# A hybrid decoder layer on one core: another order of the seven products of Strassen's scheme in the feed-forward part, with four of them summed in PSUM

## The chip, the cores and the metric

The kernel runs on 1 core of one Trainium2 chip. The metric is the device time of one execution in microseconds (us); a profile of one execution shows what each engine did. The engines are TensorE (PE; its weight loads are shown apart as PEld), VectorE (DVE), ScalarE (ACT), GpSimd (POOL) and SyncE (SP, which issues most transfers).

## The reference

One decoder layer on 512 positions of width 2048, in float32. The token mixers in the first half are not touched by the change; the feed-forward part is.

```python
D_MODEL, SEQ = 2048, 512
D_FF = 5632                         # -(-(8 * D_MODEL) // (3 * 256)) * 256
def reference(...):
    h = _rms_norm(x, norm1_g[l])
    proj = h @ w_in[l]
    ...                             # three causal token mixers: out_a, out_b, out_c
    x = x + jnp.concatenate([out_a, out_b, out_c], axis=-1) @ w_out[l]
    h2 = _rms_norm(x, norm2_g[l])
    x = x + (jax.nn.silu(h2 @ w_gate[l]) * (h2 @ w_up[l])) @ w_down[l]
```

## The kernel before

**Stages.** The input projection and the mixers come first, then the output projection, then an Up phase (gate and up) and a Down phase. All matrix products run in three passes: each float32 operand is split into a high part of reduced precision (`wh`, `high`) and the rest (`wl`, `low`), and high x high, high x low and low x high are summed in PSUM.

**Output projection.** It takes 32 units of work, each with one weight tile of 128x1024 and 24 matmuls of 512 columns. A unit writes one of two PSUM banks (pool `tiles`); `residual` (L1098) adds the bank to the residual `xr` on DVE. With each finished row of x, small steps follow by a clock of ticks: the square on ACT (L1118) and its sum `ssum` on DVE (L97), and the halves of the normalised activations, their differences and sums (`ta`, `tb`, `h`, L1128 to L1148), which the Up phase multiplies. The last unit of the output projection is unit -1 here, the one ahead of it -2, and so on.

**Up and Down.** Both use a scheme of seven products in place of eight (Strassen's, in Winograd's form): the weights are cut into four quarters 11, 12, 21, 22, the activations likewise, and seven products of sums of quarters give the four quarters c00, c01, c10, c11 of the result. Up has 11 blocks of two sub-blocks, u0 to u21; one sub-block computes its seven products in the order of `ORDER`, each in two units A and B of 12 matmuls. The result quarters with first index 1 are the gate, those with 0 are up. Down has 12 blocks d0 to d11, of seven products too; where a range has three columns of blocks instead of four, the block is narrower (18 matmuls to a product instead of 24). A product fills two PSUM banks; there are two such pairs of banks, taken in turn, and the list `(7, 1, 5, 2)` says which products start a sum there afresh. A product outside the list adds to what is in its pair: 4 to product 7, 6 to product 1, 3 to product 5. `done` then tells what is read from the banks after each product and added to which result quarter; DVE does most of it, `six` reads product 6's sum three times.

**Weight sums.** Five sums of weight quarters are made on POOL by `plus` (L172), each in the raw buffers that the quarters were loaded to: s = 21 + 11; 21 = 21 + 22; 11 = 21 + 11 (with the new 21); and later 11 = 11 + 12, so four sums for each of A and B. The table `sums` puts each of them at the start of a numbered unit, counted from the first unit `base` of the sub-block. `entries` is the order of the loads, `bufs` says which raw buffer each quarter takes, and `pump` issues the next load as soon as its buffer is free. `works` is the order in which units use them. Two units ahead of its use, a quarter is split: ACT makes a rounded copy in PSUM (`wn`, L283) and one in SBUF (`wh`, L284), DVE subtracts (`wl`, L285). For the weights of the output projection DVE subtracts a copy in SBUF (L263).

The order of the work on each engine is that in which the program is written; no scheduler moves it.

## Time and profile before

| | |
|---|---|
| Time, median of 3 runs | 1843.49 us (1842.29 to 1843.87) |
| Span of the profiled execution | 1840.0 us |
| Its own time beside the span | not given apart; the median lies 3.49 us above the span |
| Output projection's last unit | 571.06 to 576.50 us |
| Up phase | 576.50 to 1414.30 us |
| Down phase | from 1414.30 us to near the end |

How its lines are read: a row of a timeline gives the start, the length, the engine, the line of the program, the operation, output <- inputs, and in brackets the idle time before it with what ended it. A group's row gives the count, the busy time, the mean of one in ns, and the idle time ahead. A row of windows gives the stretch, its length, each engine's busy time with its instructions, then the granted clock of PE, the share of the DMA engines and GB/s.

### The profile page before, as it was taken

To read this page: it belongs to the slowest core of one execution; us is meant where nothing else is said; L and a number is where in the kernel's file an instruction comes from. 1 tells how busy PE (TensorE), PEld (TensorE's weight loads), DVE (VectorE), ACT (ScalarE), POOL (GpSimd) and SP (SyncE) were. 2 spreads that over 40 slices of the span, in tenths; PEclk is the share of its full clock that TensorE was granted. 3 is DMA by queue.
4 is the path that set the end of the run, shared out by engine and by line. 5 is a ranking of instruction groups with operands and counts; after the bars stand their busy time and mean duration, and the time that the engine had idled before them with its cause. 6 is when DMAs were issued, how large, how long until landed. Compare 5 with 4: busy or idle time off the path is not lost.

```text
span 1840.0 us, 26561 instructions
## 1 busy us (share of the span) xinstructions
PE 1832.2 (100%) x8314; PEld 1521.0 (83%) x8314; DVE 1430.0 (78%) x2023; ACT 1313.4 (71%) x1784; POOL 1019.0 (55%) x793
## 2 busy tenths in 40 slices
PE   9999999999999999999999999999999999999998
PEld 7888888888888888888888888888888888888887
DVE  6689888986689877777777777777777777777777
ACT  6355644553468788887888888888887778877775
POOL 0126543110003557886887767787776558776552
PEclk9999999999999999999999999999999999999999
DMA  7353255363343466777867778677687579877635
GB/s 276 88 150 121 88 145 156 107 178 132 118 138 104 115 160 183 203 205 183 227 179 210 209 185 224 174 207 210 178 273 255 200 232 294 252 259 259 237 121 109
DMA packets 401612, 337.81 MB, mean 184 GB/s; under 512 B 185408, under 2 KB 327872, under 8 KB 401472
## 3 DMA queue, kind: packets, MB, share of 16 engines
q1 hardware_dynamic: 400896, 335.33, 62.9%
q8 instruction: 66, 1.08, 0.2%
q10 hardware_dynamic: 576, 0.79, 0.1%
q14 instruction: 74, 0.61, 0.1%
HBM read 261.61 MB, written 66.03 MB: 178 GB/s over the span
## 4 chain that ended last, share of the span: by engine, by line
PE 73%; DVE 1%; DMA 0%; issue 0%; ACT 0%; DVEq 0%; SPq 0%
PE out L1307 15%; PE out L1304 15%; PE out L1306 15%; PE out L1570 7%; PE out L1569 7%; PE out L1571 7%; PE o L322 2%; PE o L324 2%; PE o L323 2%; DVE y L1579 0%; DVE wl L285 0%; DMA out_T<-z 0%; DVE z L1478 0%; DVE lnv L412 0%; DVE y L1548 0%
## 5 line engine op out<-in xcount | busy, mean ns | idle before, releaser
L1304 PE MATMUL out<-wh,h 128*128 128x512 f32 x1232 | 479.2, 389 | 0.0
L1306 PE MATMUL out<-wl,h 128*128 128x512 f32 x1232 | 479.2, 389 | 0.0
L1307 PE MATMUL out<-wh,h 128*128 128x512 f32 x1232 | 479.2, 389 | 0.0
L1306 PEld LDWEIGHTS out<-wl,h 128*128 128x128 f32 x1232 | 231.2, 188 | 48.1
L1307 PEld LDWEIGHTS out<-wh,h 128*128 128x128 f32 x1232 | 231.2, 188 | 48.1
L1304 PEld LDWEIGHTS out<-wh,h 128*128 128x128 f32 x1232 | 231.2, 188 | 47.9
L1570 PE MATMUL out<-wl,a 128*128 128x512 f32 x620 | 240.4, 388 | 0.1
L1569 PE MATMUL out<-wh,a 128*128 128x512 f32 x620 | 240.4, 388 | 0.0
L1571 PE MATMUL out<-wh,a 128*128 128x512 f32 x620 | 240.3, 388 | 0.0
L289 ACT CAST wh<-w 128x1024 fp32r<-128x1024 f32 (+2 forms) x94 | 97.0, 1031 | 134.3 <-PE o L323 46.0
L1579 DVE TENSOR_TENSOR y<-y,out 128x512 f32<-128x512 f32 x192 | 128.4, 684 | 46.8 <-PE out L1571 45.0
L263 DVE TENSOR_TENSOR wl<-w,wh 128x1024 fp32r<-128x1024 f32 (+2 forms) x95 | 114.4, 1204 | 34.0 <-ACT wh L289 33.8
L1570 PEld LDWEIGHTS out<-wl,a 128*128 128x128 f32 x620 | 116.4, 188 | 24.2 <-DVE wl L285 0.5
L1569 PEld LDWEIGHTS out<-wh,a 128*128 128x128 f32 x620 | 116.4, 188 | 24.1
L1571 PEld LDWEIGHTS out<-wh,a 128*128 128x128 f32 x620 | 116.4, 188 | 23.8
L573 DVE SCALAR_TENSOR_TENSOR y<-bu,cst,y 128x511 f32<-128x511 f32 (+14 forms) x120 | 88.9, 741 | 1.1
L322 PE MATMUL o<-mh_c,wh 128*128 128x512 f32 x128 | 51.0, 398 | 0.0
L322 PE MATMUL cq<-hh,wh 128*128 128x512 f32 x128 | 50.3, 393 | 0.0
L324 PE MATMUL o<-mh_c,wl 128*128 128x512 f32 x128 | 50.0, 391 | 0.0
L323 PE MATMUL o<-ml_c,wh 128*128 128x512 f32 x128 | 50.0, 390 | 0.0
L323 PE MATMUL cq<-hl,wh 128*128 128x512 f32 x128 | 49.9, 390 | 0.0
L324 PE MATMUL cq<-hh,wl 128*128 128x512 f32 x128 | 49.9, 390 | 0.0
(2353 smaller groups left out, 4745.0 us busy)
## 6 DMA issues: line engine op xcount, KB each, us to landing
od<-a SPq DMA_DIRECT2D x154, 256.0 KB
a<-od SPq DMA_DIRECT2D x154, 256.0 KB
w<-in_wi SPq DMA_DIRECT2D x58, 512.0 KB
w<-in_wo SPq DMA_DIRECT2D x32, 512.0 KB
x<-in_xT SPq DMA_DIRECT2D x16, 256.0 KB
xr<-in_xT SPq DMA_DIRECT2D x16, 256.0 KB
x2d<-xr SPq DMA_DIRECT2D x16, 256.0 KB
z<-x2d SPq DMA_DIRECT2D x64, 64.0 KB
```

The lines of the kernel that those rows point to most:

```text
L263: fn(*args)
L289: (nc.vector.tensor_copy if u == 0 else nc.scalar.copy)(hi[:, :n], t[:, :n])
L322: nc.tensor.matmul(out, wh, xh, start=start, stop=False)
L323: nc.tensor.matmul(out, wh, xl, start=False, stop=False)
L324: nc.tensor.matmul(out, wl, xh, start=False, stop=stop)
L1304: nc.tensor.matmul(b, x[:, high], wh[:, s], start=c == f == 0 and q in (7, 1, 5, 2), stop=False, skip_group_check=True)
L1306: nc.tensor.matmul(b, x[:, high], wl[:, s], start=False, stop=False, skip_group_check=True)
L1307: nc.tensor.matmul(b, x[:, low], wh[:, s], start=False, stop=c == f == 1, skip_group_check=True)
L1569: nc.tensor.matmul(b[:, lo:hi], x[:, high], wh[:, s], start=start, stop=False, skip_group_check=True)
L1570: nc.tensor.matmul(b[:, lo:hi], x[:, high], wl[:, s], start=False, stop=False, skip_group_check=True)
L1571: nc.tensor.matmul(b[:, lo:hi], x[:, low], wh[:, s], start=False, stop=last, skip_group_check=True)
L1579: getattr(eng, op)(t, t, src)
```

## The change

`ORDER` becomes 1, 7, 6, 4, 5, 2, 3, and only 1, 7 and 2 start afresh. So 6 is summed onto 1 in the same banks, 4 onto 7, 5 onto 1 + 6, and, after 2 in the other pair, 3 onto 1 + 6 + 5. Each pair of banks is read once after each product: `six` and, in Down, `copy_u` with its subtraction on POOL go away; c10 takes product 6's sum with a minus sign. The weight sums are placed anew: s three units ahead of the sub-block instead of four, 21 two units ahead instead of at its start, 11 one ahead instead of two behind; the last sum stays at the eighth unit. The loads come in the order 11, 21, 22, 12 instead of 21, 11, 22, 12, the buffers are shared out in another way, and 12 is loaded only once s has been made. Near the end of Down the transposes of result c10 come after product 4 instead of 6.

```diff
-ORDER = (7, 1, 4, 6, 5, 2, 3)
+ORDER = (1, 7, 6, 4, 5, 2, 3)
+FRESH = (1, 7, 2)
...
-    bufs = {"A": dict(zip(("21", "11", "s", "22"), ("21a", "22a", "sa", "22b"))),
-            "B": dict(zip(("21", "11", "s", "22"), ("21b", "11", "12", "sb")))}
+    bufs = {"A": dict(zip(("11", "21", "22", "s"), ("21b", "22a", "sa", "22b"))),
+            "B": dict(zip(("11", "21", "22", "s"), ("21a", "11", "12", "sb")))}
+
+    def use(base, size, keys, c):
+        i, key, buf = "AB".index(c), keys[c], bufs[c]["s"]
+        sums[base - 3 + i].append(plus(key["s"], key["21"], key["11"], size[c], buf))
+        sums[base - 2 + i].append(plus(key["21"], key["21"], key["22"], size[c]))
+        sums[base - 1 + i].append(plus(key["11"], key["21"], key["11"], size[c]))
+        sums[base + 7 + i].append(plus(key["11"], key["11"], key["12"], size[c]))
+
+    BLOCKS = (("11", False), ("s", True), ("11", False), ("22", True), ("21", True), ("12", True), ("11", True))
+
+    def turn_bufs():
+        return {c: {"11": b["22"], "21": b["21"], "22": b["s"], "s": b["11"]} for c, b in bufs.items()}
...
-        for k in ("21", "11", "22", "12"):
+        for k in ("11", "21", "22", "12"):
...
-            sums[base - 4 + i].append(plus(key["s"], key["21"], key["11"], 1024, bufs[c]["s"]))
-            sums[base + i].append(plus(key["21"], key["21"], key["22"], 1024))
-            sums[base + 2 + i].append(plus(key["11"], key["21"], key["11"], 1024))
-            sums[base + 7 + i].append(plus(key["11"], key["11"], key["12"], 1024))
-        works.extend((keys[c][k], last, "moves") for k, last in (
-            ("s", True), ("11", False), ("22", True), ("11", False), ("21", True), ("12", True), ("11", True)) for c in "AB")
+            use(base, {"A": 1024, "B": 1024}, keys, c)
+        works.extend((keys[c][k], last, "moves") for k, last in BLOCKS for c in "AB")
...
-        bufs = {c: {"21": b["22"], "11": b["21"], "s": b["s"], "22": b["11"]} for c, b in bufs.items()}
+        bufs = turn_bufs()
...
     def pump(limit, most=99, eng=nc.sync):
         while at["entry"] < len(entries) and len(raws) < limit and entries[at["entry"]][0] not in held and most:
+            key = entries[at["entry"]][1]
+            if isinstance(key, tuple) and key[0] == "12" and ("s", key[1]) not in made:
+                break
...
-        def six(self, by, a, b):
-            by(0, 1, a, b)
-            self.less(0, a, b)
-            self.less(1, a, b)
...
                 elif q == 6:
-                    if a:
-                        later(0, self.six, by, a, b)
-                    else:
-                        self.six(by, a, b)
+                    if first:
+                        self.keep(1, 0, a, b, -1.0)
+                    else:
+                        self.less(0, a, b)
...
-            if self.end:
-                self.less(1, 0, a, b)
-            else:
-                later(0, self.copy_u, a, b, queue=extras)
-
-        def copy_u(self, a, b):
-            u = slot(f"d{self.t}u{a}")
-            nc.scalar.copy(u, b)
-            later(0, self.less, 1, 0, a, u, nc.gpsimd)
...
-            if self.end and q == 6:
+            if self.end and q == 4:
```

How it moves instructions is seen best at three places. In the changed program the lines stand a few numbers lower down (L172 is L173 there, L285 L290, L1330 L1335, L1579 L1581 or L1585, L1478 L1480).

The first is POOL ahead of and in the first sub-block, u0. Before:

```order
L172 TENSOR_TENSOR w('s', 'u0A')_5765<-w('21', 'u0A')_5556,w('11', 'u0A')_5609 128x1024
L172 TENSOR_TENSOR w('s', 'u0B')_5814<-w('21', 'u0B')_5559,w('11', 'u0B')_5664 128x1024
L172 TENSOR_TENSOR w('21', 'u0A')_5556<-w('21', 'u0A')_5556,w('22', 'u0A')_5817 128x1024
L172 TENSOR_TENSOR w('21', 'u0B')_5559<-w('21', 'u0B')_5559,w('22', 'u0B')_5872 128x1024
L172 TENSOR_TENSOR w('11', 'u0A')_5609<-w('21', 'u0A')_5556,w('11', 'u0A')_5609 128x1024
L172 TENSOR_TENSOR w('11', 'u0B')_5664<-w('21', 'u0B')_5559,w('11', 'u0B')_5664 128x1024
```

After the change:

```order
L173 TENSOR_TENSOR w('s', 'u0A')_5818<-w('21', 'u0A')_5609,w('11', 'u0A')_5504 128x1024
L173 TENSOR_TENSOR w('21', 'u0A')_5609<-w('21', 'u0A')_5609,w('22', 'u0A')_5714 128x1024
L173 TENSOR_TENSOR w('s', 'u0B')_5873<-w('21', 'u0B')_5664,w('11', 'u0B')_5559 128x1024
L173 TENSOR_TENSOR w('11', 'u0A')_5504<-w('21', 'u0A')_5609,w('11', 'u0A')_5504 128x1024
L173 TENSOR_TENSOR w('21', 'u0B')_5664<-w('21', 'u0B')_5664,w('22', 'u0B')_5769 128x1024
L173 TENSOR_TENSOR w('11', 'u0B')_5559<-w('21', 'u0B')_5664,w('11', 'u0B')_5559 128x1024
```

The sum into 21 of A now stands ahead of s of B, and the first sum into 11 ahead of 21 of B. What the order doesn't show: s of A takes the buffer that unit -2's weights leave, s of B that of unit -1; before, these went to the two loads of 22, and s took buffers that were free earlier.

The second is DVE around product 6 in the first sub-block of an Up block (block 5; `out_5990` to `out_5993` are the four PSUM banks, `b5c` the result tiles). Before, from the reads of product 6 to those of product 5:

```order
L1330 TENSOR_TENSOR b5c_9776<-b5c_9776,out_5992 128x512
L1330 TENSOR_TENSOR b5c_9669<-b5c_9669,out_5992 128x512
L285 TENSOR_TENSOR wl_9840<-w('12', 'u10A')_9588,wn_9841 128x1024
L1319 TENSOR_SCALAR b5c_9865<-out_5993,n2w 128x512
L1330 TENSOR_TENSOR b5c_9778<-b5c_9778,out_5993 128x512
L1330 TENSOR_TENSOR b5c_9671<-b5c_9671,out_5993 128x512
L285 TENSOR_TENSOR wl_9870<-w('12', 'u10B')_9612,wn_9871 128x1024
L1330 TENSOR_TENSOR b5c_9669<-b5c_9669,out_5990 128x512
L1330 TENSOR_TENSOR b5c_9671<-b5c_9671,out_5991 128x512
```

After the change, from the read of product 6 past those of product 4 to those of product 5:

```order
L1322 TENSOR_SCALAR b5c_9735<-out_5991 128x512
L290 TENSOR_TENSOR wl_9741<-w('21', 'u10A')_9390,wn_9742 128x1024
L290 TENSOR_TENSOR wl_9772<-w('21', 'u10B')_9423,wn_9773 128x1024
L1329 TENSOR_TENSOR b5c_9733<-b5c_9733,out_5992 128x512
L1329 TENSOR_TENSOR b5c_9735<-b5c_9735,out_5993 128x512
L290 TENSOR_TENSOR wl_9798<-w('12', 'u10A')_9598,wn_9799 128x1024
L290 TENSOR_TENSOR wl_9827<-w('12', 'u10B')_9631,wn_9828 128x1024
L1335 TENSOR_TENSOR b5c_9681<-b5c_9681,out_5990 128x512
L1335 TENSOR_TENSOR b5c_9683<-b5c_9683,out_5991 128x512
```

Before, bank `out_5993` was read three times by DVE alone; now each bank has one reader (that of product 6's other bank is ACT's), and two adds follow two splits.

The third is DVE near the end, in the last Down block. Before, from the adds of product 6 (`x3`: three rows alike) to the first of product 5:

```order
L1579 TENSOR_TENSOR y<-y,out_5990 128x512 x3
L285 TENSOR_TENSOR wl_17767<-w('12', 'd11A')_17552,wn_17768 128x1024
L1478 STREAM_TRANSPOSE z_17761<-y 128x16x32
L1579 TENSOR_TENSOR y<-y,out_5991 128x512 x3
L1478 STREAM_TRANSPOSE z_17792<-y 128x16x32
L285 TENSOR_TENSOR wl_17795<-w('12', 'd11B')_17572,wn_17796 128x1024
L285 TENSOR_TENSOR wl_17817<-w('11', 'd11A')_17414,wn_17818 128x1024
L1478 STREAM_TRANSPOSE z_17792<-y 128x16x32
L1579 TENSOR_TENSOR y<-y,out_5992 128x512
```

After the change, from the adds of product 4, which has that place now, to the first of product 5:

```order
L1581 TENSOR_TENSOR y<-y,out_5990 128x512
L1581 TENSOR_TENSOR y<-y,out_5991 128x512
L290 TENSOR_TENSOR wl_17590<-w('12', 'd11A')_17418,wn_17591 128x1024
L1480 STREAM_TRANSPOSE z_17585<-y 128x16x32
L1480 STREAM_TRANSPOSE z_17612<-y 128x16x32
L290 TENSOR_TENSOR wl_17615<-w('12', 'd11B')_17438,wn_17616 128x1024
L290 TENSOR_TENSOR wl_17637<-w('11', 'd11A')_17206,wn_17638 128x1024
L1480 STREAM_TRANSPOSE z_17612<-y 128x16x32
L1585 TENSOR_TENSOR y<-y,out_5992 128x512
```

Of three adds to each bank one is left: four rows fewer ahead of the last splits.

## The prediction

> **What bounds the kernel now.** I read the page first, then the busy time by stage, then the lines that touch the change, and last the two places at which TensorE (PE) is not covered. The page:

> ```profile
> span 1840.0 us, 26561 instructions
> PE 1832.2 (100%) x8314; PEld 1521.0 (83%) x8314; DVE 1430.0 (78%) x2023; ACT 1313.4 (71%) x1784; POOL 1019.0 (55%) x793
> ```

> The span is 1840.0 us; the median of the runs, 1843.49, lies 3.49 above it, and I carry that offset unchanged. Matmuls fill the span. The busy time by stage (Up phase; Down phase to near the end; columns PE, PEld, DVE, ACT, POOL, then the granted clock):

> ```profile
> 576.50:1414.30 837.80, 837.80 (x3698) 693.71 (x3697) 643.80 (x741) 696.23 (x844) 614.16 (x420) 1.00 0.71 195
> 1414.30:1834.00 419.70, 419.51 (x1862) 347.37 (x1861) 320.72 (x382) 319.29 (x383) 265.00 (x161) 1.00 0.71 220
> ```

> In the Up phase PE has no gap at all, in the Down phase 0.2 us, at a clock of 1.00. DVE is busy 77% there, ACT 83%, POOL 73%, all beside PE. The change leaves the number of matmuls as it is, so work taken from DVE, ACT and POOL is worth nothing where PE doesn't wait; only a wait that goes or comes counts.

> **The change part by part.**

> *Fewer reads of products.* Groups and single rows of the adds:

> ```profile
> L1579 DVE TENSOR_TENSOR y<-y,out 128x512 f32<-128x512 f32 x192 | 128.4, 684 | 46.8 <-PE out L1571 45.0
> L1330 DVE TENSOR_TENSOR b1c<-b1c,out 128x512 f32<-128x512 f32 x12 | 7.8, 680 | 1.2 <-ACT b1c L1315 1.0
> 1437.26 0.57 ACT L1594 COPY d0u<-out 128x512 f32<-128x512 f32 x1
> 1437.91 1.30 POOL L1579 TENSOR_TENSOR y<-y,d0u 128x512 f32<-128x512 f32 x1 [5.80 <-ACT d0u L1594]
> ```

> Up loses 8 DVE operations per block, 11 x 8 x 0.68 = 60 us; Down loses 26 DVE adds (17.8 us), 22 ACT copies (12.5) and 22 POOL subtracts (28.6). All lay beside a full PE: price 0 but at the very end. The banks still alternate in pairs, each read while the other product's two units run, so no new bank wait arises.

> *The end.* DVE's last rows and PE's, in order of time:

> ```profile
> 1828.28 1.21 DVE L285 TENSOR_TENSOR wl<-w('11', 'd11B')_17437,wn 128x1024 fp32r<-128x1024 f32 x1
> 1829.08 0.39 PE L1569 MATMUL out<-wh,a 128*128 128x512 f32 x1
> 1829.54 0.50 PE L1570 MATMUL out<-wl,a 128*128 128x512 f32 x1
> 1829.88 0.40 PE L1571 MATMUL out<-wh,a 128*128 128x512 f32 x1
> ...
> 1831.82 0.65 DVE L1548 TENSOR_TENSOR y<-y,out 128x512 f32<-128x512 f32 x1
> 1832.52 0.44 PE L1534 MATMUL sides<-ident,y 128*128 128x128 f32 x2
> ...
> 1834.98 0.41 PE L1534 MATMUL sides<-ident,y 128*128 128x128 f32 x2 [0.60 <-DVE y L1548]
> ```

> At the pitch of 0.227 (837.8 us over 3696 matmuls: 11 blocks, 28 units, 12 each) the matmuls at 1829.54 and 1829.88 are 0.34 late, behind a weight split that DVE starts late, and the transposes at 1832.52 some 0.3 to 0.4 behind an add. In the last block DVE has four adds fewer ahead of that split (2.7 us), so both waits go: -0.7 (bounds 0 and -0.75). The last one (0.60) is a true dependence and stays.

> *The weight sums in the Up and Down phases.* They are POOL additions of 2.4 us. The new order wants the second sum into 11 made about 11.3 us after a sub-block's start T: product 6, which uses it, is moved one place ahead; its second unit starts at T + 5 x 2.72 = 13.6 and is split 2.3 earlier. The first sum can't start before T-9.1, when the previous block's last split has freed its buffer; until the second 11 sum POOL has six sums and at most a pair of gate products:

> ```profile
> 1260.45 2.41 POOL L172 TENSOR_TENSOR w('21', 'u18A')_12262<-w('21', 'u18A')_12262,w('22', 'u18A')_12478 128x1024 f32<-128x1024 f32 x1 [0.98 <-DMA w('22', 'u18A')_12478<-in_wgu]
> 1267.54 2.55 POOL L1386 TENSOR_TENSOR b8c<-b8c,b8c 128x512 f32<-128x512 f32 x2
> ```

> 6 x 2.41 + 2.55 = 17.0, so T+7.9: 3.4 us of cover. After a narrow Down block (28.56 us instead of 38.08, an estimate from 126 and 168 matmuls at 0.227) the same count, with the splits before it closer together, gives T+10.8: 0.5 of cover. Price 0, bounds 0 and +1.

> *The first sub-block.* Here the change costs. Before, its sums and the DVE rows beside them:

> ```profile
> 547.43 2.46 POOL L172 TENSOR_TENSOR w('s', 'u0A')_5765<-w('21', 'u0A')_5556,w('11', 'u0A')_5609 128x1024 f32<-128x1024 f32 x1 [68.13 <-DVE wl L263]
> 553.89 2.47 POOL L172 TENSOR_TENSOR w('s', 'u0B')_5814<-w('21', 'u0B')_5559,w('11', 'u0B')_5664 128x1024 f32<-128x1024 f32 x1 [4.00 <-DVE wl L263]
> 565.41 2.40 POOL L172 TENSOR_TENSOR w('21', 'u0A')_5556<-w('21', 'u0A')_5556,w('22', 'u0A')_5817 128x1024 f32<-128x1024 f32 x1 [9.05 <-DMA w('22', 'u0A')_5817<-in_wgu]
> 569.45 2.58 POOL L172 TENSOR_TENSOR w('21', 'u0B')_5559<-w('21', 'u0B')_5559,w('22', 'u0B')_5872 128x1024 f32<-128x1024 f32 x1 [1.64 <-DMA w('22', 'u0B')_5872<-in_wgu]
> ```

> ```profile
> 547.55 2.62 DVE L1148 TENSOR_TENSOR h<-h,h 128x256 fp32r<-128x256 f32 x1
> ...
> 553.67 0.42 DVE L1148 TENSOR_TENSOR h<-ta,h 128x256 fp32r<-128x256 f32 x1
> 554.01 2.63 DVE L1148 TENSOR_TENSOR h<-tb,h 128x256 fp32r<-128x256 f32 x1
> ...
> 559.11 1.21 DVE L263 TENSOR_TENSOR wl<-w,wh 128x1024 fp32r<-128x1024 f32 x1
> ...
> 563.36 1.22 DVE L263 TENSOR_TENSOR wl<-w,wh 128x1024 fp32r<-128x1024 f32 x1
> 565.91 1.22 DVE L285 TENSOR_TENSOR wl<-w('s', 'u0A')_5765,wn 128x1024 fp32r<-128x1024 f32 x1 [1.34 <-PE o L324]
> 567.05 1.04 DVE L1148 TENSOR_TENSOR h<-ta,h 128x256 fp32r<-128x256 f32 x1
> ...
> 569.69 0.67 DVE L1098 TENSOR_TENSOR xr<-xr,o 128x512 f32<-128x512 f32 x1
> 570.29 2.29 DVE L97 TENSOR_TENSOR ssum<-ssum,sr 128x512 f32<-128x512 f32 x1
> ```

> The reader is to see that a DVE operation with both inputs in SBUF stands still while POOL adds: 2.62 and 2.63 instead of 0.41, 2.29 instead of 0.68. One with a PSUM input doesn't: the add at 569.69 ran 0.67 inside POOL's 569.45 to 572.03, the split at 565.91 (wn is in PSUM) 1.22 inside its 565.41 to 567.81.

> In the changed order 11, 21 and 22 take the buffers that come free early, and s of A the buffer freed by the split at 559.11, s of B that of the split at 563.36. POOL's order is sA, 21A, sB, 11A, 21B, so five sums, 12 us, want POOL between about 558 and 575, where there were two; their loads landed long before. The add at 569.69 reads the one of two PSUM banks that the output projection's last unit writes next, from:

> ```profile
> 571.08 0.39 PE L322 MATMUL o<-mh_a,wh 128*128 128x512 f32 x1
> ```

> The add ended at 570.36: 0.72 of cover. Its new time: the two blockades at 547 and 554 are gone, but ACT limits what comes of it:

> ```profile
> 554.74 1.06 ACT L289 CAST wh<-w 128x1024 fp32r<-128x1024 f32 x1 [1.71 <-PE o L323]
> 555.69 0.63 ACT L1118 ACTIVATE sr<-xr 128x512 f32<-128x512 f32 x1
> ```

> DVE adds that square to ssum from 556.25 on and then starts the split of 559.11, so at 556.85, 2.26 earlier. The idle 1.34 at 565.91 and the 0.63 lost at 567.05 fill up. Against it stand four blockades of 2.2 and one (sB) of about 1.5, since DVE then is partly in a split with a PSUM input: 10.4. So 570.36 - 2.26 - 1.34 - 0.63 + 10.4 = 576.5, and PE stands for 5.4 us. Bounds: 0 if DVE goes ahead of every waiting sum, 6.0 if sB blocks fully too. I take 5.4, because in these rows POOL got in after one DVE operation each time (553.67, then 553.89). What comes behind has cover: the later sums are wanted from unit 4 on, 20 us on.

> [...]

> ```profile
> 143.41 0.85 POOL L897 TENSOR_SCALAR_AFFINE_SELECT c0pl<-c0lp 128x256 fp32r<-128x256 f32 x1 [2.77 <-DVE c0lp L888]
> ...
> 144.51 0.67 DVE L558 TENSOR_TENSOR bu<-bu,r1b 128x512 f32<-128x512 f32 x1
> 144.58 2.67 POOL L897 TENSOR_SCALAR_AFFINE_SELECT c0pl<-c0lp 128x256 fp32r<-128x256 f32 x1
> 145.11 1.20 DVE L263 TENSOR_TENSOR wl<-w,wh 128x1024 fp32r<-128x1024 f32 x1
> ```

> There POOL's operation of 0.85 took 2.67, behind at least these two DVE operations. If POOL loses like that, its sums slip to where DVE has PSUM work, and the stall shrinks.

> *The clock.* A gap of 5.4 us in PE has no precedent in the run, but its end has one:

> ```profile
> 1837.00:1837.50 0.50, 0.00 (x0) 1.00 0.73 125
> 1837.50:1838.00 0.50, 0.00 (x0) 0.68 0.83 254
> 1838.00:1838.50 0.50, 0.00 (x0) 0.50 0.79 266
> ```

> The last matmul ended at 1835.39; at about 1837.7, 2.3 us on, the granted clock was halved. No row shows how long it takes to come back; with the same 2.3 us, matmuls at half speed lose 2.3 x 0.5 = 1.15. Bounds 0 and 5.4 (the whole next unit at half speed). [...]

> Sum: 1843.49 - 0.7 + 5.4 + 1.15 = 1849.3.

> **The rivals.** (a) The stall without the fall of the clock: 1848.2. For it: the gap is only twice what the fall took at the end. (b) DVE goes ahead of some sums, as at 144.58: two to four blockades instead of five, so 4.4 to 8.8 of the 10.4 are lost, and since 2.26 + 1.34 + 0.63 + 0.72 = 4.95 are covered, PE stands 0 to 3.85: 1842.8 to 1846.6 or, if the clock falls too, 1847.8. (c) Not slower: POOL runs the sums while DVE is in operations with a PSUM input or idle, and the add slips by less than its cover. That decides at the 4.95 us of lost DVE time; then only the end is left, 1842.8. For it: I worked out the times from the order, and half a microsecond at a split moves a sum past a DVE row. Against it: DVE is busy through nearly all of this stretch, mostly with two SBUF inputs. (d) Cover is also lost behind a narrow Down block, up to three such places of 1 us: 1852. (e) Faster: the gaps of PE that the profile shows outside the start add up to under 2 us, so nothing here reaches 1839.8.

> **How the numbers follow.** A measurement tells about 0.2%, 3.7 us, from no change: 1839.8 and 1847.2. Chances: full stall with the clock 0.40 (1849.3), (a) 0.21 (1848.2), (b) 0.19, (c) 0.13, (d) 0.04, and 0.03 for faster by something the profile doesn't show. Slower: 0.40 + 0.21 + 0.04, and 0.03 of (b): 0.68. Same: 0.16 + 0.13 = 0.29. The range takes in (c) at its low end, 1842.5, and at the top the stall's 6.0 with a clock term of 3, 1851.8; the likeliest case alone holds 1848 to 1851.8.

> **What would show it.** In the changed profile: five POOL sums between 558 and 576; DVE operations with two SBUF inputs of 2.6 us, about one to each; PE waiting some 5 us for the add of xr before the last unit of the output projection; a granted clock under 1 in the slice behind it; Up phase without a gap; PE's waits of 0.34 and 0.3 at the end gone. Wrong if POOL's sums take 3 to 5 us each while DVE runs on, or if PE has a gap in Up or Down.

## The result and the profile after

| | before | after |
|---|---|---|
| Time, median | 1842.89 us (the three runs above and a fourth, 1841.96 to 1843.87) | 1935.41 us (4 runs, 1932.79 to 1936.89) |
| Ratio | | 1.0500, 95% interval 1.0485 to 1.0514 |
| Span of the profiled execution | 1840.0 us | 1935.2 us |

The change costs 92.5 us. I had forecast 1849.3 us, 1842.5 to 1851.8: the direction was right, the size was not, and most of the loss lies where I had expected none. The page after, first its span and its busy times:

```profile
span 1935.2 us, 26380 instructions
PE 1863.8 (96%) x8314; PEld 1537.5 (79%) x8314; DVE 1369.7 (71%) x1909; ACT 1301.7 (67%) x1762; POOL 988.0 (51%) x771
```

DVE, ACT and POOL do less, as intended, and PE is busy 31.6 us longer with the same 8314 matmuls: they ran slower for a time. PE's waits (total, times, longest):

```profile
PE out L1311 <- DVE wl L290: 54.7, 12, 6.4
PE o L327 <- ACT h L1147: 5.2, 1, 5.2
PE out L1309 <- ACT wh L289: 3.8, 6, 1.1
...
PE out L1571 <- ACT wh L289: 0.4, 1, 0.4
```

Together 64.1 us, of which before had none. Waits of 64.1 and slower matmuls of 31.6, less the 0.7 won at the end, make 95.0 of the span's 95.2. The second row is the stall that I forecast. The first is one that I did not: 1.5 in u0, and then, at the fourth unit of every second sub-block, 1.9 in u2, 3.0 in u4 (and 1.4 behind it), and 4.8 to 6.5 in each of the eight from u6 to u20.

2.3 us of the slower matmuls are no part of the change. They lie at the start of the program, whose first twelve matmuls of real work take 5.2 us instead of 2.9; the first four, before and after:

```profile
5.46 1.21 PE L516 MATMUL in<-hh,wh 128*128 128x512 f32 x4 [0.74 <-ACT hh L402]
5.39 2.07 PE L521 MATMUL in<-hh,wh 128*128 128x512 f32 x4 [0.67 <-ACT hh L407]
```

From there on every matmul of this execution is 2.3 us later. Of the experiments' profiled executions some begin as late or nearly so, others like the one before, so a difference of up to 2.3 us between two spans, or between the same matmul in two traces, can be this alone.

**The stall that was forecast.** POOL, DVE and PE at the end of the output projection, after the change:

```profile
560.56 2.46 POOL L173 TENSOR_TENSOR w('s', 'u0A')_5818<-w('21', 'u0A')_5609,w('11', 'u0A')_5504 128x1024 f32<-128x1024 f32 x1 [79.00 <-DMA x2d<-xr]
563.10 2.46 POOL L173 TENSOR_TENSOR w('21', 'u0A')_5609<-w('21', 'u0A')_5609,w('22', 'u0A')_5714 128x1024 f32<-128x1024 f32 x1
569.23 2.41 POOL L173 TENSOR_TENSOR w('s', 'u0B')_5873<-w('21', 'u0B')_5664,w('11', 'u0B')_5559 128x1024 f32<-128x1024 f32 x1 [3.67 <-DMA x2d<-xr]
571.58 2.58 POOL L173 TENSOR_TENSOR w('11', 'u0A')_5504<-w('21', 'u0A')_5609,w('11', 'u0A')_5504 128x1024 f32<-128x1024 f32 x1
574.11 2.52 POOL L173 TENSOR_TENSOR w('21', 'u0B')_5664<-w('21', 'u0B')_5664,w('22', 'u0B')_5769 128x1024 f32<-128x1024 f32 x1
```

```profile
560.68 2.62 DVE L1153 TENSOR_TENSOR h<-h,h 128x256 fp32r<-128x256 f32 x1
563.22 2.62 DVE L1139 TENSOR_TENSOR ta<-h,h 128x256 f32<-128x256 f32 x1
...
570.36 1.55 DVE L1153 TENSOR_TENSOR h<-ta,h 128x256 fp32r<-128x256 f32 x1
571.84 2.59 DVE L1153 TENSOR_TENSOR h<-tb,h 128x256 fp32r<-128x256 f32 x1
574.36 2.56 DVE L1153 TENSOR_TENSOR h<-h,h 128x256 fp32r<-128x256 f32 x1
...
577.84 0.67 DVE L1103 TENSOR_TENSOR xr<-xr,o 128x512 f32<-128x512 f32 x1
```

```profile
578.66 0.77 PE L327 MATMUL o<-mh_a,wh 128*128 128x512 f32 x1 [5.16 <-ACT h L1147]
```

Five sums of POOL come in the order of the program, with one gap of 3.67; to each of them belongs a DVE operation with two SBUF inputs that takes 1.6 to 2.6 us instead of 0.41. The add of `xr` (L1103, L1098 before) ends at 578.51, and PE's unit, due at 573.5, starts at 578.66: 5.16 us late. The row names ACT as the last releaser, but ACT's step had itself waited 7.2 us for DVE.

**The stall that was not.** One of the eight, at sub-block u6, whose first matmul started at T = 826.9. SyncE's queue, then POOL, DVE and PE:

```profile
814.14 2.06 SPq L1258 DMA_DIRECT2D p3r<-bd  x4
...
819.20 1.77 SPq L248 DMA_DIRECT2D w('22', 'u6A')_7992<-in_wgu  x2
821.02 5.21 SPq L1421 DMA_DIRECT2D z<-x2d  x4
```

```profile
818.68 2.43 POOL L173 TENSOR_TENSOR w('s', 'u6A')_8046<-w('21', 'u6A')_7936,w('11', 'u6A')_7877 128x1024 f32<-128x1024 f32 x1 [4.69 <-DVE wl L290]
828.64 2.40 POOL L173 TENSOR_TENSOR w('21', 'u6A')_7936<-w('21', 'u6A')_7936,w('22', 'u6A')_7992 128x1024 f32<-128x1024 f32 x1 [7.54 <-DMA z<-x2d]
831.00 2.40 POOL L173 TENSOR_TENSOR w('s', 'u6B')_8070<-w('21', 'u6B')_7969,w('11', 'u6B')_7910 128x1024 f32<-128x1024 f32 x1
...
838.01 2.50 POOL L1388 TENSOR_TENSOR b2c<-b2c,b2c 128x512 f32<-128x512 f32 x2
```

```profile
827.75 1.21 DVE L290 TENSOR_TENSOR wl<-w('s', 'u6A')_8046,wn 128x1024 fp32r<-128x1024 f32 x1
839.31 0.71 DVE L1392 STREAM_TRANSPOSE b2c<-b2c 128x512 f32<-128x512 f32 x1 [10.36 <-POOL b2c L1388]
...
841.17 1.18 DVE L290 TENSOR_TENSOR wl<-w('s', 'u6B')_8070,wn 128x1024 fp32r<-128x1024 f32 x1
```

```profile
835.48 0.49 PE L1309 MATMUL out<-wh,h 128*128 128x512 f32 x1 [0.28 <-ACT wh L289]
842.41 0.80 PE L1311 MATMUL out<-wl,h 128*128 128x512 f32 x1 [6.43 <-DVE wl L290]
```

Read from the end: PE waits 6.43 for the split of s of B (841.17). Its sum was ready at 833.40. But the split stands on DVE behind the transposes of the previous block (839.31), and DVE is idle 10.36 us for their gate product; that stands on POOL (838.01) behind the sums; and POOL had stood still for 7.54 us ahead of the sum into 21, since the load of 22 had not landed. (The row names the reads `z<-x2d`, which were issued right behind that load. In u8, u12, u14 and u16 the same wait, 6.3 to 7.1 us, is put down to the load itself.)

```profile
916.37 2.39 POOL L173 TENSOR_TENSOR w('21', 'u8A')_8663<-w('21', 'u8A')_8663,w('22', 'u8A')_8719 128x1024 f32<-128x1024 f32 x1 [7.13 <-DMA w('22', 'u8A')_8719<-in_wgu]
```

The load of 22 for u6 was issued at 819.20, behind the reads `p3r<-bd`, with the reads `z<-x2d` beside it. It is a chain over four queues (SyncE, POOL, DVE, PE), each in order. Counted from T the load was issued when it was before the change, at T - 7.7; but its sum now stands ahead of others that are wanted sooner, and it landed later: from issue to sum 9.4 us instead of 6.0, and 7.3 to 9.4 instead of 5.7 to 6.1 in the eight sub-blocks.

**The clock** behind this wait, in stretches of 1 us (columns: length, PE busy and matmuls, granted clock, DMA share, GB/s):

```profile
839.00:840.00 1.00, 0.00 (x0) 0.96 0.00 0
840.00:841.00 1.00, 0.00 (x0) 0.50 0.11 41
...
846.00:847.00 1.00, 1.00 (x4) 0.62 0.41 129
```

PE stopped at 835.98; the clock fell to half at about 839.9 and came back at about 846.8, 4.3 us after PE had started again. So this wait of 6.4 us cost about 2 more (4.3 at half clock). It fell so at each of the nine longest waits (the stall ahead of u0, and u6 to u20), and was at half for 3.2 to 5.9 us behind them. It also fell for 3.4 us behind the wait of 1.9 in u2, though not at that of 3.0 in u4. In all, resumed work ran at half clock for 48 us, which costs 24 of the 31.6 us; 2.3 more are the program's start, and the rest I have not placed.

**The end** went as forecast; both waits are gone (1829.54 and 1832.52 before):

```profile
1924.20 0.39 PE L1573 MATMUL out<-wh,a 128*128 128x512 f32 x1
1924.42 0.39 PE L1571 MATMUL out<-wh,a 128*128 128x512 f32 x1
...
1927.78 0.28 PE L1573 MATMUL out<-wh,a 128*128 128x256 f32 x1
1927.90 0.38 PE L1536 MATMUL sides<-ident,y 128*128 128x128 f32 x2
```

The matmuls keep their pitch of 0.227, the transposes follow after 0.12.

### The profile page after: what moved, and what is told of

The parts are those of the page before. It is cut to its first block, busy times and chain, and to the rows that moved or that the text cites. A ratio compares the mean times of both kernels' runs of the same rounds, so it can differ in the third digit from the quotient of the medians.

```text
span 1935.2 us, 26380 instructions
## 1 busy us (share of the span) xinstructions
PE 1863.8 (96%) x8314; PEld 1537.5 (79%) x8314; DVE 1369.7 (71%) x1909; ACT 1301.7 (67%) x1762; POOL 988.0 (51%) x771
## 4 chain that ended last, share of the span: by engine, by line
PE 50%; ACT 5%; POOL 5%; SPq 5%; issue 4%; DMA 4%; DVE 2%; POOLq 0%; DVEq 0%; ACTq 0%
PE out L1311 8%; PE out L1312 8%; PE out L1309 8%; PE out L1571 7%; PE out L1573 7%; PE out L1572 7%; ACT wh L289 2%; ACT wn L288 2%; PE o L327 2%; PE o L328 2%; PE o L329 2%; SPq L1421 2%; DVE wl L290 1%; SPq L248 1%; SPq L1242 1%
## 5 line engine op out<-in xcount | busy, mean ns | idle before, releaser
L1311 PE MATMUL out<-wl,h 128*128 128x512 f32 x1232 | 490.2, 398 | 54.7 <-DVE wl L290 54.7
L1309 PE MATMUL out<-wh,h 128*128 128x512 f32 x1232 | 487.6, 396 | 3.8 <-ACT wh L289 3.8
L1312 PE MATMUL out<-wh,h 128*128 128x512 f32 x1232 | 486.8, 395 | 0.0
L1311 PEld LDWEIGHTS out<-wl,h 128*128 128x128 f32 x1232 | 236.3, 192 | 109.9 <-DVE wl L290 60.1
L1309 PEld LDWEIGHTS out<-wh,h 128*128 128x128 f32 x1232 | 235.8, 191 | 57.2 <-ACT wh L289 7.4
L1312 PEld LDWEIGHTS out<-wh,h 128*128 128x128 f32 x1232 | 236.5, 192 | 49.1
L1571 PE MATMUL out<-wh,a 128*128 128x512 f32 x620 | 240.5, 388 | 0.4 <-ACT wh L289 0.4
L1571 PEld LDWEIGHTS out<-wh,a 128*128 128x128 f32 x620 | 116.4, 188 | 24.6 <-ACT wh L289 0.9
L1581 DVE TENSOR_TENSOR y<-y,out 128x512 f32<-128x512 f32 x118 | 80.0, 685 | 33.7 <-PE out L1573 31.2
```

The lines of the kernel that those rows point to most:

```text
L1309: nc.tensor.matmul(b, x[:, high], wh[:, s], start=c == f == 0 and q in FRESH, stop=False, skip_group_check=True)
L1311: nc.tensor.matmul(b, x[:, high], wl[:, s], start=False, stop=False, skip_group_check=True)
L1312: nc.tensor.matmul(b, x[:, low], wh[:, s], start=False, stop=c == f == 1, skip_group_check=True)
L1571: nc.tensor.matmul(b[:, lo:hi], x[:, high], wh[:, s], start=start, stop=False, skip_group_check=True)
```

## The experiments

Each ratio is to runs of the kernel before that were taken beside the experiment's. In diffs, lines are those of the changed kernel unless told otherwise.

### The first sub-block's sums as before

```diff
-    bufs = {"A": dict(zip(("11", "21", "22", "s"), ("21b", "22a", "sa", "22b"))),
-            "B": dict(zip(("11", "21", "22", "s"), ("21a", "11", "12", "sb")))}
+    bufs = {"A": dict(zip(("11", "21", "22", "s"), ("21b", "22a", "22b", "sa"))),
+            "B": dict(zip(("11", "21", "22", "s"), ("21a", "11", "sb", "12")))}
...
-            use(base, {"A": 1024, "B": 1024}, keys, c)
+            use(base, {"A": 1024, "B": 1024}, keys, c, *([(-4, 0, 2)] if n == 0 else []))
```
(the three numbers are the units, from `base`, at which `use` places s, 21 and the first sum into 11)

> The changed kernel with the sums and buffers of the first sub-block alone placed as before the change. Theory (the stall ahead of the output projection's last unit comes from five sums on POOL that block DVE): the gap of 5.2 us and the half clock behind it, 5.2 us at half speed, go: 5.2 + 2.6 = 7.8 us less, 1927.6 us. Rival (the stall there has another cause, such as ACT): no change, 1935 us.

1933.16 us, ratio 1.0491 (1.0475 to 1.0506). The wait of 5.2 us and the half clock behind it are gone, so its cause is shown: the place of u0's sums. The same matmul late in u0 starts 7.0 us earlier (597.86 instead of 604.88), 2.3 of them from the program's start, although a wait of 3.66 now stands there instead of one of 1.49. The clock falls behind that wait, for 3.4 us. At the end 2.3 us are left instead of the 7.8 that I expected, and the intervals don't tell that from none.

### The sums where they were before, with the new order of products

```diff
-        sums[base - 3 + i].append(plus(key["s"], key["21"], key["11"], size[c], buf))
-        sums[base - 2 + i].append(plus(key["21"], key["21"], key["22"], size[c]))
-        sums[base - 1 + i].append(plus(key["11"], key["21"], key["11"], size[c]))
+        sums[base - 4 + i].append(plus(key["s"], key["21"], key["11"], size[c], buf))
+        sums[base + i].append(plus(key["21"], key["21"], key["22"], size[c]))
+        sums[base + 2 + i].append(plus(key["11"], key["21"], key["11"], size[c]))
```
(with the buffers and the order of the loads of the kernel before)

> The changed kernel's products, accumulation and reads, but the weight sums, loads and buffers placed as before the change (s four units ahead, 21 at the start, 11 two units behind). Theory A (the schedule of the sums costs all): no wait for s or behind the gate products; only the second sum into 11 is now late for product 6, done at about T+12.6 where its split should start at T+11.3: 1 to 2 us in each of 11 even sub-blocks, no fall of the clock, so 1850 to 1865 us. Rival B (reading each bank once, or the new order of accumulation, costs by itself): the waits stay, over 1900 us.

1941.93 us, 1.0534 (1.0519 to 1.0550): slower than the change itself. My theory as put down was wrong here, for the waits only changed place. PE's waits, then u6 on POOL:

```profile
PE out L1309 <- ACT wh L289: 64.6, 16, 7.2
```

```profile
837.86 2.34 POOL L173 TENSOR_TENSOR w('11', 'u6A')_7936<-w('21', 'u6A')_7877,w('11', 'u6A')_7936 128x1024 f32<-128x1024 f32 x1
```

Now product 6 waits, for the first sum into 11: it starts at 837.86, behind the sums into 21 that wait for 22, the gate products and more, and product 6 comes 5.4 us earlier in a sub-block than it did. So the old places, as they are, don't serve the new order. The time is in rival B's range, but B isn't shown by it: nothing here waits for a read of a bank, and the best version below keeps the new order and its reads and lies 5.3 us above the kernel before.

### The gate products on DVE

```diff
-                nc.gpsimd.tensor_mul(t, t, self.c[1, k, a])
+                nc.vector.tensor_mul(t, t, self.c[1, k, a])
```

> The changed kernel with the gate products (4 of 128x512 in a block) on DVE instead of POOL. Theory A1 (in each even sub-block PE waits for the split of s of B, which stands on DVE behind transposes that wait for a gate product, which stands on POOL behind sums that wait for the load of 22): the waits of 5 to 6.5 us shrink to what the second sum into 11 is late, under 2 us, and the clock doesn't fall: 54.7 us of waits become under 20 and 25 us of slow matmuls go, so 1855 to 1885 us. Rival A2 (the sums themselves are late, the gate products are innocent): waits stay, over 1920 us.

1892.42 us, 1.0268 (1.0251 to 1.0285): 43 us less than the change.

```profile
PE out L1309 <- ACT wh L289: 16.8, 17, 1.5
PE out L1311 <- DVE wl L290: 9.6, 7, 3.0
```

The waits of 5 to 6.5 us in Up are gone, 26 us in smaller ones are left, and 14 us of the slow matmuls went (PE busy 1849.5), 2.3 of them at the program's start. The gate product's place was a link of the chain, as theory A1 has it, though the time lies 7 us above its range. It is a costly cure: on DVE two of them, with both inputs in SBUF, took 4.81 us beside POOL's sums (two took 2.50 on POOL in the changed kernel):

```profile
824.16 4.81 DVE L1388 TENSOR_TENSOR b2c<-b2c,b2c 128x512 f32<-128x512 f32 x2
```

### Gate product ahead of the sums that wait for 22

```diff
-        sums[base - 2 + i].append(plus(key["21"], key["21"], key["22"], size[c]))
-        sums[base - 1 + i].append(plus(key["11"], key["21"], key["11"], size[c]))
+        sums[base + i].append(plus(key["21"], key["21"], key["22"], size[c]))
+        sums[base + 1 + i].append(plus(key["11"], key["21"], key["11"], size[c]))
```

> The changed kernel with the sum into 21 two units later and the first sum into 11 two units later, so that POOL makes s of A and B and the first gate product before it waits for the load of 22; loads, buffers and DVE's order unchanged. Theory A1: the transposes no longer wait, the split of s of B is in time; instead the second sum into 11 comes behind the second gate product, at about T+13 where T+11.3 is wanted: waits of 2 to 3 us in the even sub-blocks, which is too short for the clock to fall, 1865 to 1885 us. Theory A3 alone (all that matters is that 22 lands late): no gain, 1930 us or more.

1929.73 us, 1.0470 (1.0454 to 1.0486). The waits for the split of s are gone, but most of their time came back as waits of product 6, two to a sub-block, for both sums into 11; 5.7 us less than the change is close to the "no gain" of theory A3 alone:

```profile
PE out L1309 <- ACT wh L289: 44.2, 21, 4.1
```

I had counted only the second one, and had taken waits of 2 to 3 us as too short for the clock; that of 3.0 in u4 of the changed kernel had not brought it down, but that of 1.9 in u2 had. At u6 each of two, of 2.6 and 2.5 us with 4.6 us of work between them, brought it down for 3.4 us; in all of Up it fell at least 14 times. So none of the three orders of POOL's work tried here gives enough cover, as long as 22 lands late.

### The reads of the gated blocks three units later

```diff
-                first, every, more = {NBLOCKS - 2: (52, 16, 4), NBLOCKS - 1: (56, 16, 4)}.get(self.n, (5, 13, 0))
+                first, every, more = {NBLOCKS - 2: (52, 16, 4), NBLOCKS - 1: (56, 16, 4)}.get(self.n, (8, 13, 0))
```

> The changed kernel with only the reading of the gated blocks (p..l, p..r from bd, on SyncE's queue) three units later, as in the run with the late transposes, but the transposes where the change has them. Theory A1 (the transposes stand ahead of the split of s of B on DVE, and wait for the gate product): the transposes' place is what counts, so waits of 4 us or more stay, 1915 to 1935 us. Theory A3 (the load of 22 is late because it stands behind those reads on SyncE; with it in time the sums, the gate product and the transposes all are): the waits go, 1855 to 1870 us. In between: both.

1880.64 us, 1.0205 (1.0190 to 1.0221): 54.8 us less than the change. SyncE, POOL and DVE at u6, where T is 821.3, and PE's waits:

```profile
808.93 1.89 SPq L248 DMA_DIRECT2D w('22', 'u6A')_7977<-in_wgu  x2
...
815.71 2.99 SPq L1258 DMA_DIRECT2D p3r<-bd  x4
```

```profile
817.57 2.42 POOL L173 TENSOR_TENSOR w('21', 'u6A')_7918<-w('21', 'u6A')_7918,w('22', 'u6A')_7977 128x1024 f32<-128x1024 f32 x1
...
827.72 2.57 POOL L1388 TENSOR_TENSOR b2c<-b2c,b2c 128x512 f32<-128x512 f32 x2
```

```profile
829.08 0.71 DVE L1392 STREAM_TRANSPOSE b2c<-b2c 128x512 f32<-128x512 f32 x1 [3.28 <-POOL b2c L1388]
...
830.96 1.18 DVE L290 TENSOR_TENSOR wl<-w('s', 'u6B')_8066,wn 128x1024 fp32r<-128x1024 f32 x1
```

```profile
PE out L1311 <- DVE wl L290: 22.4, 11, 2.2
```

The load of 22 now stands ahead of `p3r<-bd` and is issued at T - 12.3 instead of T - 7.7, POOL's sum into 21 starts without a wait at T - 3.7 instead of T + 1.8, and each of ten waits, u2 to u20, is at most 2.2 us. The clock falls behind only two of them, in u2 and in u16, for 3.4 us each (PE busy 1843.0, 20.8 less, 2.3 of that at the program's start). The one in u16, whose wait ends at 1225.81, in stretches of 1 us:

```profile
1227.00:1228.00 1.00, 1.00 (x5) 0.58 1.07 357
1228.00:1229.00 1.00, 1.00 (x4) 0.50 0.75 157
```

What is left of each wait is the second link: DVE's split still stands behind the transposes. Both theories hold, A3 for the larger part; the time lies between their two ranges.

### The transposes three units later too

```diff
-                later(2, self.turn, q - 2)
-                later(3, self.store, q - 2, queue=extras)
+                later(5, self.turn, q - 2)
+                later(6, self.store, q - 2, queue=extras)
```
(with the reads of the gated blocks three units later, which these need)

> The changed kernel with DVE's transposes of the gated blocks three units later (and their store and the reading of it), POOL unchanged. Theory A1: the split of s of B no longer waits, but the second sum into 11 still stands behind the gate product on POOL, done at T+15.3 where T+11.3 is wanted: a wait of 3 to 4.5 us instead of 5 to 6.5, 1890 to 1915 us. If DVE's order alone were the cause: under 1870 us. Rival A2: no change, over 1930 us.

1857.34 us, 1.0077 (1.0062 to 1.0092). I had expected the second sum into 11 to stay late, because I had not seen that the reads, moved with the transposes, let 22 land earlier; the run above shows that part apart. Against that run it wins 23.3 us, which the place of the transposes (and of the store behind them) is worth. Of PE's longer waits one is left:

```profile
PE o L327 <- ACT h L1147: 5.2, 1, 5.2
```

All ten are gone; the stall ahead of u0 and five short ones, 5.0 us together, are left.

### Both, and the first sub-block

Late transposes and reads, and u0's sums as before:

> Late transposes (and their reading) together with the first sub-block's sums and buffers as before the change. Of the 14 us that late transposes left over the kernel before, the stall at the output projection's last unit is 5.2 us and its half clock 2.6: without them 1849 to 1851 us. If the first sub-block's stall only moves to a later wait, as with its sums alone placed as before (3.7 us behind the first sub-block's product 4): 1853 to 1856 us.

1853.25 us, 1.0056 (1.0039 to 1.0073), in the second of the ranges expected. The stall of 5.2 us is gone, and a wait of 3.66 came up behind it in u0, with a half clock of 3.4 us. DVE and PE there:

```profile
591.76 2.62 DVE L1153 TENSOR_TENSOR h<-tb,h 128x256 fp32r<-128x256 f32 x1
...
597.17 1.21 DVE L290 TENSOR_TENSOR wl<-w('22', 'u0A')_5817,wn 128x1024 fp32r<-128x1024 f32 x1
```

```profile
598.43 0.80 PE L1311 MATMUL out<-wl,h 128*128 128x512 f32 x1 [3.66 <-DVE wl L290]
```

A DVE operation of 0.41 takes 2.62 beside POOL's sum of 11 and 12 for B (591.51 to 594.11), and what follows on DVE, up to the split of 22 that PE waits for, is late. So, in addition, those two sums of u0 on DVE:

```diff
-            nc.gpsimd.tensor_add(out[:, :n], raws[a][0][:, :n], raws[b][0][:, :n])
+            eng.tensor_add(out[:, :n], raws[a][0][:, :n], raws[b][0][:, :n])
```
(with `eng=nc.vector` for the sums of 11 and 12 in u0)

> As the run with late transposes and the first sub-block's sums as before the change, and in that first sub-block the two sums of 11 and 12 on DVE instead of POOL. Theory (the wait of 3.7 us that is left in the first sub-block comes from DVE's operations with two SBUF inputs standing still for 2.6 us behind those sums on POOL, and half a clock of 3.8 us follows it): 3.7 + 1.9 less, 1847 to 1849 us. Rival (DVE is simply behind there, and two more operations of 1.2 us on it make it no better): 1852 to 1855 us.

1848.39 us, 1.0027 (1.0016 to 1.0038), 4.9 us less; PE's wait for the split of 22 is 0.80 there instead of 3.66.

```profile
PE out L1311 <- DVE wl L290: 1.6, 3, 0.8
```

So 87 of the 92.5 us are found, each by the experiment that takes it away, in this order: 54.8 for the reads ahead of the load of 22, 23.3 for the transposes, 4.1 and 4.9 for u0's sums. (In another order the shares differ: the first step for u0 gave 2.3 by itself, 4.1 behind the others.) This is the best version with the new order that I ran; it doesn't beat the kernel before, and 5.3 us stay. 2.3 of them are short waits, these and one of 0.7 in d4. Matmul by matmul against the kernel before, this execution loses 2.3 us at the program's start, 2.5 in u0 and 1.0 at the wait in d4; the rest comes in small steps that I have not traced.

### A control

The kernel before, with its transposes, stores and reads three units later, by the same edit:

> A control: the kernel before the change, with the transposes of the gated blocks, their store and their reading three units later. If the late place only takes away a wait that the change made, this one stays within 0.2% of the kernel before, 1840 to 1846 us. If the late place is worth something by itself: under 1839 us.

1842.66 us, 0.9999 (0.9989 to 1.0009). The late place is worth nothing by itself; it mends what the change broke.

## Why the prediction was right or wrong

**The first sub-block: right.** Five sums, one blocked DVE operation to each, PE 5.16 us late where I had 5.4. The add of `xr` ends at 578.51, or 576.2 without the 2.3 of the program's start, where the sum had 576.5. Beside each of the five a DVE operation with two SBUF inputs took 1.6 to 2.6 us instead of 0.41, while the sums took 2.41 to 2.58, as before the change (2.40 to 2.58); the row at 144.58 in the run before, in which POOL's operation was the long one (2.67 instead of 0.85), had no second one here.

**The clock: the fall right, its price too small.** At the first stall it fell 3.6 us after PE's last matmul (573.5 to 577.1) and stayed at half until 583.9, 5.3 us after the restart, so 2.6 us instead of 1.15. The time to come back, which I had put equal to the 2.3 us that the clock took to fall at the end of the run before, was the wrong part: behind the long waits of this trace it fell 2.5 to 5.2 us after the stop and came back 3.2 to 5.9 after the restart. A wait shorter than any of these times brought it down too, that of 1.9 us in u2. The clock term of 3 at the top of my range comes from no row of a run; 2.6 was measured in its place.

**The end: right.** The waits of 0.34 and 0.3 to 0.4 are gone, the one of 0.6 stayed.

**The reads of the products: right.** In no run does PE wait in Up or Down for a read of a product.

**The weight sums in Up: wrong, and with it the forecast.** The step that failed is "6 x 2.41 + 2.55 = 17.0, so T+7.9: 3.4 us of cover", with its price of 0 and bounds of 0 and 1. The start of it, T - 9.1, was right (T - 8.2 at u6). But the sum ran POOL's work through without a gap, while the second of the six sums needs the load of 22. The row that I quoted for the length of a sum says so itself, `[0.98 <-DMA w('22', 'u18A')_12478<-in_wgu]`: it starts at 1260.45, and u18 began at 576.50 + 18 x 38.08 = 1261.94, so 22 had landed only at T - 1.5. With that alone, the five sums from there on and a pair of gate products end at T - 1.5 + 5 x 2.41 + 2.55 = T + 13.1, past the T + 11.3 of the deadline: no cover at all. In the changed trace 22 lands later still, and at u6 the sum into 21 starts at T + 1.8. Before the change that sum stood behind s of both halves and the first gate product, so its wait held up nothing.

Second, I treated the gate products as 2.55 us of POOL time and did not ask who waits for them. DVE's transposes do, and the splits that PE needs stand behind those. I had walked such a chain through for the output projection and not for the sub-blocks behind it, where a wait counts ten times. What had the price 0 came to 58.9 us of waits (the first, third and fourth row of PE's waits) and some 21 us of half clock behind them.

So the direction came out right by a step that makes some 8 of the 92.5 us, the first stall and its clock. The rest is what the forecast itself had named as a sign of being wrong, gaps of PE in Up.

Of the rivals only (d) lay near, at 1 us and three places behind narrow Down blocks. PE waits at one of them, 0.43 us in d4.

## What to carry to other kernels

Before a piece of work is moved ahead in an in-order queue, look up in the trace when each of its inputs lands, not only when its output buffer comes free: the bracket of its own row tells. If it then waits, everything behind it on that queue waits too, and so does whatever stands behind the readers of that on the next queue (at u6 7.54 us on POOL, then 10.36 on DVE, then 6.43 on PE). Walk that through first in the stage that repeats most.

## What the runs showed of the hardware that I had not expected

A short wait brought the clock down as well in some places, and its length alone did not tell whether it would. Of the ten waits of 1.75 to 2.2 us with the late reads, some 79 us apart, two did. Eleven of 1.77 to 2.72 us with the gate product first, in u6 to u18 and mostly in pairs with some 4.5 us of work between, all did. One of 3.0 us, in u4 of the changed kernel, did not. Of that kernel's other waits in Up none of up to 1.5 us did, and all from 4.8 us on did.

And the same load of 512 KB took a different time: that of 22 for u6 took 9.4 us from its issue to the sum that waited for it in the changed kernel, 6.0 before (797.26 to 803.22). How much of that is the small reads beside it was not tried apart.
